# Linear ReLU attention on one core: the first octet's K loaded as 256 pieces of 4 KB into the halves of two output buffers

## The chip, the core and the metric

The kernel runs on one core of one Trainium2 chip. The metric is the device time of one execution in microseconds (us); of three runs the median is 125.16 us (125.11 to 125.23). The core has a matrix engine (PE, with its weight loads PEld), a vector engine (DVE), a scalar engine (ACT), GpSimd (POOL) and a sync engine (SP), and 16 DMA engines that move data between the HBM and the on-chip memory. That memory has 128 partitions. SP and POOL issue all transfers of this kernel, each on a queue of its own; the 16 DMA engines serve both queues.

## The reference

For each of 8 x 12 = 96 heads, with 512 rows of 64 numbers in Q, K and V:

```python
Q_feat = np.maximum(0, Q)
K_feat = np.maximum(0, K)
KV = np.einsum('bhkd,bhkv->bhdv', K_feat, V)
K_sum = np.sum(K_feat, axis=2)
numerator = np.einsum('bhqd,bhdv->bhqv', Q_feat, KV)
denominator = np.einsum('bhqd,bhd->bhq', Q_feat, K_sum)
return (numerator / (denominator[:, :, :, None] + 1e-10)).astype(np.float32)
```

Inputs and output are fp32, 12.58 MB each.

## The kernel before

The heads are taken eight at a time: 12 octets, each 1 MB of Q, K, V and output. An octet of an input is one contiguous megabyte in the HBM; it is laid on the 128 partitions as 128 rows of 2048 fp32, so a partition holds 32 sequence rows of one head (16 partitions for each head).

**Loads.** Of octets 1 to 11, and of octet 0's Q, every load is issued by POOL (`load`, line 171, the transfer on line 174) and converts to bf16 on the way, into rings of six slots for each of Q, K and V (`NI = 6`). Octets 2 to 9 are loaded two at a time, the others singly. Six semaphore lanes (`LANES`) limit how many loads POOL has under way, so POOL runs ahead of the engines that use the data. Octet 0's K and V are the exception: `body` (lines 265 to 267) has SP load them first of all, in fp32, into the output buffers `o_sb[0]` and `o_sb[1]`, which hold no output yet. `kv_src` (line 166) tells the steps that prepare K and V where an octet lies.

**Compute.** For each octet DVE makes `kf` from K (`prep_k`, line 187: the maximum with zero, and a mask that keeps the heads apart), DVE and ACT make `vo` from V (`prep_v`, line 194), and DVE copies Q (`copy_q`). PE transposes Q, sums K against V over 64 matmuls (line 412), multiplies with Q (line 381) and transposes the result back (line 421). DVE scales it by the reciprocal denominators into an output buffer (`norm`, line 241). Octet o's output goes to buffer (o + 2) mod 10 of the ten (`NOUT = 10`) 8 KB buffers.

**Stores.** SP issues the 12 stores of 1 MB (`store`, line 248). Each also waits for the last K load (line 252), so no store starts before all K loads have landed. Those of octets 0 to 3 are issued at the step of octet 4, each later one at the end of its octet's step. After the last store SP waits until its data has landed (line 433), which ends the program.

**Order.** Class `Order` (line 9) keeps, for every buffer key such as `("o", 0)` or `("k", 3)`, its last writer and its readers, and turns them into semaphore waits. The order of instructions on each engine is the order in which `body`, `setup`, `begin` and `step` write them.

Of the kernel before, what the change touches and what calls it, by code (L numbers as in the profile page):

```python
# [96 lines left out]
def kernel(  # L97
# [8 lines left out]
    B, H, S, D = Q.shape  # L106
    assert D == 64
    P = 128
# [3 lines left out]
    R = S * 4 // P  # L112
    RQ = S * 8 // P
# [3 lines left out]
    NI = 6  # L117
    NOUT = 10
    LANES = 6

    fp32 = mybir.dt.float32
    bf16 = mybir.dt.bfloat16
    Act = mybir.ActivationFunctionType
    Alu = mybir.AluOpType

    sb = ctx.enter_context(tc.tile_pool(name="sb", bufs=1))
    psum = ctx.enter_context(tc.tile_pool(name="psum", bufs=1, space=bass.MemoryType.PSUM))

    def view(X, f):
        return X.rearrange("b h s d -> (b h s d)").rearrange("(n p f) -> n p f", p=P, f=f)  # L130

    Qr, Kr, Vr, Or = [view(X, RQ * D) for X in (Q, K, V, out)]
# [3 lines left out]
    mask = sb.tile([P, 2, 2], fp32, name="mask")  # L136
    mask_h = sb.tile([P, 8, 2], fp32, name="mask_h")
    kf = sb.tile([P, RQ, 2, D], bf16, name="kf")
    vo = sb.tile([P, RQ, 2, D4], bf16, name="vo")
# [6 lines left out]
    den = sb.tile([P, RQ], fp32, name="den")  # L146
    rec = sb.tile([P, RQ], fp32, name="rec")
    ins = {n: sb.tile([P, NI, RQ * D], bf16, name=f"{n}_sb") for n in "qkv"}
    o_sb = [sb.tile([P, RQ, D], fp32, name=f"o_sb{i}") for i in range(NOUT)]
    ps_kv = psum.tile([P, 2, 512], fp32, name="ps_kv")  # L150
    ps_den = ps_kv[:, 1, 256:512]
    ps_qt = [psum.tile([P, U // 2, P], bf16, name=f"ps_qt{j}") for j in range(2)]
# [7 lines left out]
    def lane(who):  # L160
        turn[who] += 1
        return lanes[who][(turn[who] - 1) % len(lanes[who])]

    do = Order(nc, sems)

    def kv_src(o):
        if o == 0:
            return (o_sb[0], ("o", 0)), (o_sb[1], ("o", 1))
        return [(ins[n][:, o % NI].rearrange("p (r d) -> p r d", d=D), (n, o % NI)) for n in "kv"]

    def load(n, *octets):
        o, i, m = octets[0], octets[0] % NI, len(octets)
        src = {"q": Qr, "k": Kr, "v": Vr}[n][o:o + m].rearrange("n p f -> p n f")
        do.op("pool", lambda e: e.dma_start(out=ins[n][:, i:i + m], in_=src, single_packet=True),  # L174
              writes=[(n, x % NI) for x in octets], dma=lane("pool"))

    def load_two(o):
        if o < NO - 2:
            load("q", o, o + 1)
            load("k", o, o + 1)  # L180
            load("v", o, o + 1)
        else:
            for x in (o, o + 1):
                for n in "kqv":
                    load(n, x)

    def prep_k(o, s, halves=(0, 1), after=()):
        src, key = kv_src(o)[0]
        rs = slice(R * halves[0], R * halves[-1] + R)
        do.op("dve", lambda e: e.tensor_scalar(kf[:, rs, s, :], src[:, rs], scalar1=0.0, scalar2=mask[:, 0, s:s + 1],  # L190
                                               op0=Alu.max, op1=Alu.mult),
              reads=[key, ("mask", 0), *after], writes=[("kf", s, j) for j in halves])

    def prep_v(o, t, halves, who, sem=None):
        src, key = kv_src(o)[1]
        rs = slice(R * halves[0], R * halves[-1] + R)
        to, src, m = vo[:, rs, t, 2:D + 2], src[:, rs], mask[:, 1, t:t + 1]
        if who == "act":
            make = lambda e: e.activation(to, src, Act.Copy, scale=m)  # L199
        else:  # L200
            make = lambda e: e.tensor_scalar(to, src, scalar1=m, scalar2=None, op0=Alu.mult)  # L201
        do.op(who, make, reads=[key, ("mask", 1), "vo1"], writes=[("vo", t, j) for j in halves], sem=sem)

    def copy_q(o):
        do.op("dve", lambda e: e.tensor_copy(q2.rearrange("p u f -> p (u f)"), ins["q"][:, o % NI]),  # L205
# [33 lines left out]
        do.op("dve", lambda e: e.reciprocal(rec, den), reads=["den"], writes=["rec"])  # L239

    def norm(o, j):
        i = (o + 2) % NOUT
        rs = slice(16 * j, 16 * j + 16)
        do.op("dve", lambda e: e.tensor_tensor(o_sb[i][:, rs], ps_x[j].rearrange("p (r d) -> p r d", d=D),  # L244
                                               rec[:, rs].unsqueeze(2).to_broadcast([P, 16, D]), op=Alu.mult),
              reads=[("x", j), "rec"], writes=[("o", i, j)] if i > 1 else [("o", i, j), ("o", i)], sem=f"n{j}")

    def store(o):
        i = (o + 2) % NOUT
        to, src = Or[o], o_sb[i].rearrange("p r d -> p (r d)")  # L250
        keys = [("o", i, h) for h in range(2)]
        keys.append(("k", (NO - 1) % NI))
        do.op("sp", lambda e: e.dma_start(out=to, in_=src), reads=keys,
              dma=lane("sp" if o + NOUT < NO else "last"), kept=o + NOUT >= NO)
# [6 lines left out]
    def memset(who, ap, value, key):  # L261
        do.op(who, lambda e: e.memset(ap, value), writes=[key] if isinstance(key, (str, tuple)) else key)  # L262

    def body():
        for c, X in enumerate((Kr, Vr)):
            do.op("sp", lambda e: e.dma_start(out=o_sb[c].rearrange("p r d -> p (r d)"), in_=X[0]),
                  writes=[("o", c)], dma=lane("sp"))
        load("q", 0)
        memset("pool", ident, 0.0, "ident")
        do.op("pool", lambda e: e.affine_select(out=ident, in_=ident, compare_op=Alu.not_equal, fill=1.0, base=0,  # L270
                                                pattern=[[-1, P]], channel_multiplier=1),
              reads=["ident"], writes=["ident"])
        for n in "kqv":
            load(n, 1)
        ones = vo[:, :, :, 1:D4 - 1]
        for c in range(4):
            memset("pool", ones[:, 8 * c:8 * c + 8, :, 0:D + 2:D1], 0.0, "vo1")
        for h in range(4):
            for c in range(4):
                memset("pool", ones[32 * h:32 * h + 32, 8 * c:8 * c + 8, h % 2, 0:D + 2:D1], 1.0, "vo1")  # L280
        for h in range(4):
            for t in range(2):
                memset("pool", mask[32 * h:32 * h + 32, 1, t:t + 1], 1.0 if h % 2 == t else 0.0,
                       [("m", h, t), ("mask", 1)])
        setup()
        load_two(2)
        load_two(4)
        begin()
        for o in range(NO):
            step(o)  # L290
        for n in lanes["pool"] + lanes["sp"]:
            nc.gpsimd.wait_ge(sems[n], do.count[n])
        nc.gpsimd.drain()

    def setup():
        do.op("dve", lambda e: e.tensor_copy(ident32, ident), reads=["ident"], writes=["ident32"])
        for c in range(2):
            do.op("dve", lambda e: e.tensor_reduce(
                out=mask_h[:, :, c], in_=ident32.rearrange("p (h b) -> p h b", h=8), op=Alu.add,
                axis=mybir.AxisListType.X), reads=["ident32"], writes=[("mh", c), "mask_h"])  # L300
        do.op("dve", lambda e: e.tensor_reduce(
            out=mask[:, 0, :], in_=mask_h[:, :, 0].rearrange("p (a s) -> p s a", s=2), op=Alu.add,
            axis=mybir.AxisListType.X), reads=["mask_h"], writes=[("mask", 0)])
        prep_k(0, 0)
        prep_k(0, 1)
        prep_v(0, 1, (0,), "act", "a0")
        prep_v(0, 0, (0, 1), "dve", "d0")
        prep_v(0, 1, (1,), "dve", "d1")
        do.op("dve", lambda e: e.memset(kvf.bitcast(fp32)[:, 0:4 * D1], 0.0), writes=KVD, sem="n0")
        do.op("dve", lambda e: e.memset(kvf.bitcast(fp32)[:, 4 * D1:], 0.0), writes=KVD, sem="n1")  # L310
        copy_q(0)
        for who, e, names in (("act", nc.scalar, ("t0", "t1", "rq", "ev")), ("dve", nc.vector, ("n0", "n1"))):
            for n in names:
                e.sem_inc(sems[n], 1)
                do.note(who, who, (), (), n, 1)
# [9 lines left out]
    def prepare(o):  # L325

        copy_q(o)
        for j in range(2):
            prep_k(o, 0, (j,))
            prep_k(o, 1, (j,), ["rec"] if j == 0 else [])  # L330

    def begin():
        transposed(1)
        relu_q(0)
        relu_q(1)
        summed(1)
        evac_kv()
        prep_v(1, 1, (0,), "act", "a0")
        prepare(1)

    def step(i):
# [25 lines left out]
        for j in range(2):  # L367
            norm(i, j)
        if i % 2 == 0 and i + 6 < NO:
            load_two(i + 6)  # L370
            if i + 8 == NO:
                for x in range(i):
                    store(x)
        if i + 8 >= NO:
            store(i)
# [50 lines left out]
    with tc.tile_critical(no_gpsimd_drain=True):  # L426
        body()
        products()
# [34 lines left out]
```

## Time and profile before

| what | value |
|---|---|
| median of three runs | 125.16 us |
| the profiled execution: its own time, its span | 125.21 us, 123.4 us |
| HBM read and written | 37.75 MB, 12.58 MB (408 GB/s over the span) |
| DVE, PE, ACT, POOL busy share of the span | 69%, 66%, 62%, 18% |
| POOL's queue: packets, share of the 16 DMA engines' time | 4704, 71.8% |
| SP's queue: packets, share of the 16 DMA engines' time | 2016, 28.5% |
| octet 0's K, issue to landing | 6.4 us |
| octet 0's V, issue to landing | 10.9 us |
| `prep_k` of octet 0 on DVE | 2 instructions, 2.48 us |

The span is what the profiler saw between the first and the last instruction; the execution's own time has 1.8 us more around it. "Busy" is time in which an engine executed something. The GB/s of the page count the bytes as they arrive: a load that converts 8 KB of fp32 to 4 KB of bf16 counts as 4 KB, so 214 GB/s of such loads read 428 GB/s from the HBM.

The records of single DMA packets in the trace give the size, start and duration of each row moved. SP's rows are 8192 bytes, POOL's 4096 bytes as written. Each of the 16 engines also writes a 4-byte packet to a semaphore when its part of a transfer is done.

### The profile page before, as it was taken

How to read it: one execution, taken by the hardware profiler on the slowest of the kernel's cores; microseconds unless marked ns; L12 is line 12 of the kernel's file. 1: busy time of each engine (PE TensorE's matmuls, PEld its weight loads, DVE VectorE, ACT ScalarE, POOL GpSimd, SP SyncE). 2: the span in 40 equal slices, each digit the busy share in tenths (PEclk: the TensorE clock that was granted, in tenths of full speed). 3: DMA queues.
4: the chain of work that ended last, by engine and by line, in shares of the span. 5: the costliest groups of instructions: out<-in, count | busy, mean ns of one | idle time of the engine just before them, and what ended most of it. 6: DMA issues, size and time to landing. Idle time of an engine off the chain costs nothing.

```text
span 123.4 us, 3445 instructions
## 1 busy us (share of the span) xinstructions
PE 81.2 (66%) x1440; PEld 72.4 (59%) x1440; DVE 85.7 (69%) x149; ACT 76.2 (62%) x108; POOL 21.6 (18%) x56
## 2 busy tenths in 40 slices
PE   0000088793579999898959889597999989390000
PEld 0000077693269789797939789495978977290000
DVE  1252936626975999999989899898999956733000
ACT  0000755991099697999859995799999896300000
POOL 5887922102022022010110110200000000000000
PEclk9999999999756999999999999999999999959555
DMA  2999999999999999999999999999999999999990
GB/s 72 393 313 234 212 214 214 212 212 216 216 212 215 215 216 214 212 216 214 212 215 215 215 215 214 214 215 214 212 324 421 425 425 427 422 425 425 430 425 35
DMA packets 6724, 32.55 MB, mean 264 GB/s; under 512 B 576, under 2 KB 576, under 8 KB 4928
## 3 DMA queue, kind: packets, MB, share of 16 engines
q0 software_dynamic: 4704, 17.83, 71.8%
q1 hardware_dynamic: 2016, 14.68, 28.5%
q8 instruction: 1, 0.02, 0.1%
q14 instruction: 3, 0.02, 0.0%
HBM read 37.75 MB, written 12.58 MB: 408 GB/s over the span
## 4 chain that ended last, share of the span: by engine, by line
DMA 43%; DVE 11%; PE 11%; POOL 11%; issue 9%; ACT 5%; POOLq 0%; DVEq 0%; SPq 0%
DMA v_sb<-in_V_dram 24%; DMA q_sb<-in_Q_dram 20%; DVE o_sb L244 7%; PE ps_x L421 5%; PE ps_kv L412 5%; POOL vo L262 5%; POOL q_sb L174 2%; POOL k_sb L174 2%; DVE vo L201 2%; ACT ot_sb L225 2%; ACT qt L209 1%; DVE own L230 1%; ACT kvd L217 1%; POOL v_sb L174 1%; ACT vo L199 1%
## 5 line engine op out<-in xcount | busy, mean ns | idle before, releaser
L244 DVE TENSOR_TENSOR o_sb<-ps_x,rec 128x1024 f32<-128x1024 f32 x24 | 28.5, 1219 | 5.6 <-PE ps_x L421 5.1
L412 PE MATMUL ps_kv<-vo,kf 64*128 64x132 bf16 x768 | 26.9, 229 | 7.0 <-ACT vo L199 3.5
L412 PEld LDWEIGHTS ps_kv<-vo,kf 64*128 64x128 bf16 x768 | 24.9, 99 | 10.2 <-ACT vo L199 7.8
L421 PE MATMUL ps_x<-ident,ot_sb 128*128 128x128 f32 x192 | 25.4, 289 | 1.7 <-DVE ot_sb L225 1.7
L209 ACT ACTIVATE qt<-ps_qt 128x1024 bf16<-128x1024 bf16 x24 | 23.5, 1040 | 2.1 <-PE ps_qt L388 2.1
L421 PEld LDWEIGHTS ps_x<-ident,ot_sb 128*128 128x128 f32 x192 | 22.6, 149 | 3.3 <-issue 2.2
L388 PE MATMUL ps_qt<-ident,q 128*128 128x128 bf16 x192 | 13.5, 226 | 16.2 <-DVE q L205 15.9
L225 ACT COPY ot_sb<-ps_x 128x1024 f32<-128x1024 f32 x23 | 22.2, 1015 | 2.9 <-PE ps_x L381 2.6
L190 DVE TENSOR_SCALAR kf<-k_sb,mask 128x1024 bf16<-128x1024 bf16 x44 | 19.2, 491 | 6.0 <-DMA k_sb<-in_K_dram 3.5
L388 PEld LDWEIGHTS ps_qt<-ident,q 128*128 128x128 bf16 x192 | 12.2, 101 | 16.5 <-issue 16.3
L217 ACT CAST kvd<-ps_kv 64x260 bf16<-64x260 f32 x48 | 18.0, 375 | 2.2 <-PE ps_kv L412 1.4
L199 ACT ACTIVATE vo<-v_sb,mask 128x1024 bf16<-128x1024 bf16 x11 | 12.7, 1154 | 10.1 <-DMA v_sb<-in_V_dram 9.9
L381 PE MATMUL ps_x<-qt,kvd 128*128 128x256 bf16 x96 | 13.7, 281 | 3.7 <-DVE o_sb L244 3.7
L201 DVE TENSOR_SCALAR vo<-v_sb,mask 128x2048 bf16<-128x2048 bf16 (+1 forms) x22 | 12.6, 617 | 1.3 <-DMA v_sb<-in_V_dram 1.3
L381 PEld LDWEIGHTS ps_x<-qt,kvd 128*128 128x128 bf16 x96 | 8.0, 99 | 6.2 <-DVE o_sb L244 5.0
L205 DVE COPY q<-q_sb 128x2048 bf16<-128x2048 bf16 x12 | 8.1, 674 | 2.1 <-PE ps_qt L388 2.1
L199 ACT ACT_TABLE_LOAD x1 | 1.3, 1283 | 12.4 <-DMA o_sb<-in_V_dram 12.4
L174 POOL DMA_DIRECT2D q_sb<-in_Q_dram x8 | 5.2, 655 | 18.1 <-DMA k_sb<-in_K_dram 8.7
L174 POOL DMA_DIRECT2D k_sb<-in_K_dram x7 | 5.0, 713 | 18.4 <-DMA q_sb<-in_Q_dram 10.1
L174 POOL DMA_DIRECT2D v_sb<-in_V_dram x7 | 4.8, 679 | 19.1 <-DMA v_sb<-in_V_dram 14.5
L381 PE MATMUL ps_kv<-kvd,qt 128*128 128x16 bf16 x192 | 7.0, 179 | 1.3 <-ACT kvd L217 1.3
L381 PEld LDWEIGHTS ps_kv<-kvd,qt 128*128 128x128 bf16 x192 | 6.1, 96 | 2.2 <-ACT kvd L217 2.1
(20 smaller groups left out, 29.5 us busy)
## 6 DMA issues: line engine op xcount, KB each, us to landing
out_dram<-o_sb SPq DMA_DIRECT2D x12, 1024.0 KB, 15.2
q_sb<-in_Q_dram POOLq DMA_DIRECT2D x4, 1024.0 KB, 26.6
k_sb<-in_K_dram POOLq DMA_DIRECT2D x4, 1024.0 KB, 27.9
v_sb<-in_V_dram POOLq DMA_DIRECT2D x4, 1024.0 KB, 29.1
q_sb<-in_Q_dram POOLq DMA_DIRECT2D x4, 512.0 KB, 15.2
k_sb<-in_K_dram POOLq DMA_DIRECT2D x3, 512.0 KB, 19.3
v_sb<-in_V_dram POOLq DMA_DIRECT2D x3, 512.0 KB, 15.5
o_sb<-in_K_dram SPq DMA_DIRECT2D x1, 1024.0 KB, 6.4
```

What stands on the lines that cost most here:

```text
L174: do.op("pool", lambda e: e.dma_start(out=ins[n][:, i:i + m], in_=src, single_packet=True), writes=[(n, x % NI) for x in octets], dma=lane ...
L190: do.op("dve", lambda e: e.tensor_scalar(kf[:, rs, s, :], src[:, rs], scalar1=0.0, scalar2=mask[:, 0, s:s + 1], op0=Alu.max, op1=Alu.mult) ...
L199: make = lambda e: e.activation(to, src, Act.Copy, scale=m)
L201: make = lambda e: e.tensor_scalar(to, src, scalar1=m, scalar2=None, op0=Alu.mult)
L209: do.op("act", lambda e: e.activation(qt[:, j * (U // 2):(j + 1) * (U // 2)], ps_qt[j], Act.Relu), reads=[("pq", j)], writes=[("qt", j)], ...
L217: do.op("act", lambda e: e.copy(kvd[64 * c:64 * c + 64, s:8:2, c * D1:c * D1 + D1].rearrange("p (g t) d -> p g t d", t=2), ps_kv[64 * s:64 ...
L225: do.op(who, lambda e: e.copy(to, src) if who == "act" else e.tensor_copy(to, src), reads=[("x", j)], writes=[("ot", j)], sem=f"t{j}")
L244: do.op("dve", lambda e: e.tensor_tensor(o_sb[i][:, rs], ps_x[j].rearrange("p (r d) -> p r d", d=D), rec[:, rs].unsqueeze(2).to_broadcast( ...
L381: return pe.matmul(out_, lhsT, rhs, start=True, stop=True, skip_group_check=True)
L388: x = pe.transpose(ps_qt[u // 8][:, u % 8, :], q2[:, u, :], ident)
L412: x = pe.matmul(ps_kv[:, h, 0:2 * (D + 2)].rearrange("p (t d) -> p t d", t=2), kf[ps, R * g + k, :, :].rearrange("p s d -> p (s d)"), vo[p ...
L421: x = pe.transpose(ps_x[u // 8][:, u % 8 * P:u % 8 * P + P], ot[:, u].rearrange("p h c -> p (h c)"), ident32)
```

## The change

Octet 0's K goes to the first 4 KB of output buffer 0 and the first 4 KB of output buffer 1, instead of the whole of buffer 0: each partition's 8 KB is cut into two halves of 1024 fp32. V moves from buffer 1 to buffer 2. For this the ten buffers become one tile. `prep_k` reads its source as halves `j`, for octet 0 from the two buffers, for the others from the ring slot as before. The outputs move on by one buffer, to (o + 3) mod 10, and the extra key that orders an output behind octet 0's inputs is now on buffers 0 to 2. In the built program the K transfer's memory side has 256 rows of 1024 fp32, and its on-chip side 128 x 2 x 1024; before, both had 128 rows of 2048.

```diff
-    o_sb = [sb.tile([P, RQ, D], fp32, name=f"o_sb{i}") for i in range(NOUT)]
+    o_all = sb.tile([P, NOUT, RQ * D], fp32, name="o_sb")
+    o_sb = [o_all[:, i].rearrange("p (r d) -> p r d", d=D) for i in range(NOUT)]
+
+    k_first = o_all[:, 0:2, 0:R * D]
...
     def kv_src(o):
         if o == 0:
-            return (o_sb[0], ("o", 0)), (o_sb[1], ("o", 1))
-        return [(ins[n][:, o % NI].rearrange("p (r d) -> p r d", d=D), (n, o % NI)) for n in "kv"]
+            return (k_first, [("o", 0), ("o", 1)]), (o_sb[2], [("o", 2)])
+        return (ins["k"][:, o % NI].rearrange("p (j f) -> p j f", j=2), [("k", o % NI)]), (
+            ins["v"][:, o % NI].rearrange("p (r d) -> p r d", d=D), [("v", o % NI)])
...
     def prep_k(o, s, halves=(0, 1), after=()):
-        src, key = kv_src(o)[0]
-        rs = slice(R * halves[0], R * halves[-1] + R)
-        do.op("dve", lambda e: e.tensor_scalar(kf[:, rs, s, :], src[:, rs], scalar1=0.0, scalar2=mask[:, 0, s:s + 1],
-                                               op0=Alu.max, op1=Alu.mult),
-              reads=[key, ("mask", 0), *after], writes=[("kf", s, j) for j in halves])
+        src, keys = kv_src(o)[0]
+        js = slice(halves[0], halves[-1] + 1)
+        to = kf.rearrange("p (j r) s d -> p j r s d", j=2)[:, js, :, s, :]
+        do.op("dve", lambda e: e.tensor_scalar(to, src[:, js].rearrange("p j (r d) -> p j r d", d=D), scalar1=0.0,
+                                               scalar2=mask[:, 0, s:s + 1], op0=Alu.max, op1=Alu.mult),
+              reads=[*keys, ("mask", 0), *after], writes=[("kf", s, j) for j in halves])
...
     def norm(o, j):
-        i = (o + 2) % NOUT
+        i = (o + 3) % NOUT
...
-              reads=[("x", j), "rec"], writes=[("o", i, j)] if i > 1 else [("o", i, j), ("o", i)], sem=f"n{j}")
+              reads=[("x", j), "rec"], writes=[("o", i, j)] if i > 2 else [("o", i, j), ("o", i)], sem=f"n{j}")
...
     def store(o):
-        i = (o + 2) % NOUT
+        i = (o + 3) % NOUT
...
     def body():
-        for c, X in enumerate((Kr, Vr)):
-            do.op("sp", lambda e: e.dma_start(out=o_sb[c].rearrange("p r d -> p (r d)"), in_=X[0]),
-                  writes=[("o", c)], dma=lane("sp"))
+        do.op("sp", lambda e: e.dma_start(out=k_first, in_=Kr[0].rearrange("p (j f) -> p j f", j=2)),
+              writes=[("o", 0), ("o", 1)], dma=lane("sp"))
+        do.op("sp", lambda e: e.dma_start(out=o_all[:, 2], in_=Vr[0]), writes=[("o", 2)], dma=lane("sp"))
```

More of the change, by code (lines that the diff above doesn't have):

```diff
@@ L187, in prep_k @@
     def prep_k(o, s, halves=(0, 1), after=()):
-        src, key = kv_src(o)[0]
-        rs = slice(R * halves[0], R * halves[-1] + R)
-        do.op("dve", lambda e: e.tensor_scalar(kf[:, rs, s, :], src[:, rs], scalar1=0.0, scalar2=mask[:, 0, s:s + 1],
-                                               op0=Alu.max, op1=Alu.mult),
-              reads=[key, ("mask", 0), *after], writes=[("kf", s, j) for j in halves])
+        src, keys = kv_src(o)[0]
[4 more added lines that the diff above has]
+              reads=[*keys, ("mask", 0), *after], writes=[("kf", s, j) for j in halves])
     def prep_v(o, t, halves, who, sem=None):
-        src, key = kv_src(o)[1]
+        src, keys = kv_src(o)[1]
         rs = slice(R * halves[0], R * halves[-1] + R)
@@ L201, in prep_v @@
             make = lambda e: e.tensor_scalar(to, src, scalar1=m, scalar2=None, op0=Alu.mult)
-        do.op(who, make, reads=[key, ("mask", 1), "vo1"], writes=[("vo", t, j) for j in halves], sem=sem)
+        do.op(who, make, reads=[*keys, ("mask", 1), "vo1"], writes=[("vo", t, j) for j in halves], sem=sem)
     def copy_q(o):
```

## The prediction

> **What bounds the kernel now.** First I read the table of busy time by stretches, cut where the character of the transfers changes. Its columns are the stretch, its length, busy time and instructions of PE, PEld, DVE, ACT and POOL, the granted clock, the DMA share and GB/s.
>
> ```profile
> 0.00:2.00 2.00, 0.00 (x0) 0.00 (x0) 0.00 (x0) 0.00 (x0) 0.76 (x5) 1.00 0.07 8
> 2.00:3.00 1.00, 0.00 (x0) 0.00 (x0) 0.23 (x2) 0.00 (x0) 0.92 (x4) 1.00 0.54 188
> 3.00:5.00 2.00, 0.00 (x0) 0.00 (x0) 0.73 (x3) 0.00 (x0) 1.89 (x6) 1.00 0.99 410
> ...
> 10.00:80.00 70.00, 54.11 (x994) 48.49 (x996) 55.50 (x100) 52.19 (x74) 13.88 (x30) 0.95 1.06 214
> ...
> 92.00:120.00 28.00, 15.83 (x244) 13.71 (x241) 15.43 (x25) 12.31 (x18) 0.00 (x0) 0.84 1.01 425
> 120.00:121.00 1.00, 0.00 (x0) 0.00 (x0) 0.00 (x0) 0.00 (x0) 0.00 (x0) 0.50 0.51 213
> 121.00:122.00 1.00, 0.00 (x0) 0.00 (x0) 0.00 (x0) 0.00 (x0) 0.00 (x0) 0.50 0.10 41
> ```
>
> From 3 to 120 us the DMA engines never rest, while no compute engine is full. The trace's packet records say the same row by row: each engine starts a new 8 KB row of SP's every 306 ns, and a new POOL row every 308 ns (104 starts in 2 us over 16 engines). An engine has (2 + 12) x 8 = 112 SP rows and 34 x 8 = 272 POOL rows: 112 x 0.306 + 272 x 0.308 = 118 us. Begun at about 2.6 us, that ends at 120.6. So it does: most engines end between 120.3 and 121.1, and two stragglers at 121.71 and 121.98. The last landing is at 122.45, and the span ends 1.0 us later.
>
> Next, who waits at the end, and where the compute chain takes its time from: the SP queue's waits and the chain of waits.
>
> ```profile
> SPq L434 <- DMA out_dram<-o_sb: 9.2, 1, 9.2
> ```
> ```profile
> 48.72 29.06 DMA v_sb<-in_V_dram
> 77.78 0.02 issue
> 77.80 1.16 ACT vo L199
> ```
>
> Compute waits for a V load until 77.78 us, so its clock is set there by the transfers, whatever happened at the start. And SP sits 9.2 us behind the last store. That store is issued at 112.39. The first store took 3.2 us from its issue (87.63) to its first row (90.88), with other rows ahead of it; 3.2, eight rows (2.45) and 0.46 to land make 118.5 us, against 122.45. So compute has 3.9 us to spare at the end. **The end is the start of the first rows plus all rows of the slowest DMA engine.** The change can move either of these two.
>
> **Part 1: the issue of K.** What stands ahead of the first row:
>
> ```profile
> 0.96 0.39 SPq L266 DMA_DIRECT2D o_sb<-in_K_dram  x1
> 1.40 0.42 SPq L266 DMA_DIRECT2D o_sb<-in_V_dram  x1
> ```
>
> SP issues K from 0.96 to 1.35. First rows appear at 1.98 to 2.09 on four engines and at 2.58 to 2.90 on the other twelve. POOL's rows follow only at 5.35. Until the first rows nothing covers the issue: a longer one moves all work of the DMA engines. How much longer for 256 pieces? The nearest rows are POOL's issues of one octet (128 rows) and of two (256 pieces):
>
> ```profile
> 3.71 0.55 POOL L174 DMA_DIRECT2D v_sb<-in_V_dram  x1
> ...
> 11.85 0.71 POOL L174 DMA_DIRECT2D q_sb<-in_Q_dram  x1
> ```
>
> They give +0.16 us for 128 more pieces, or a factor of 1.29, which on 0.386 us is +0.11. The bounds: nothing, if the first pieces leave while the others are being made, and +0.39, if the whole issue doubles. Below nothing it can hardly go, as K's issue does strictly more. I take +0.20, a little above POOL's row, for a reason in the built program. There 13 of SP's 14 transfers (V and the stores) have the same two-dimensional pattern on both sides and carry a mark of a pattern prepared ahead; K had both and loses both, with 256 x 1024 on one side and 128 x 2 x 1024 on the other. What SP then has to work out itself no row here shows, so the choice is mine and the bounds stay. V's issue comes later by as much; it is covered, since V's first row is due only after K's eight rows (2.45 us).
>
> [...]
>
> **Part 2: the pieces on the DMA engines.** Eight rows of 8 KB on each engine become 16 pieces of 4 KB; the bytes are the same. The 4-byte semaphore packet of SP's queue gives the fixed part of a packet: 9 ns (beside rows of 309) while SP's rows run alone, 22 ns (beside rows of 322) when they alternate with POOL's. A line through 4 bytes and 8192 bytes puts a 4 KB piece at 159 or 172 ns, so two pieces cost 9 or 22 ns more than the row. Times eight: +0.07 or +0.18 us on each engine, the bounds. Fifteen of 16 engines finish K before POOL's rows arrive, so I take a value near the first, +0.09. The Trainium skill, "DMA: Bandwidth & Descriptors", section "Why small descriptors are slow (HBM only)", states about 3 cycles over 32-byte beats for each packet: 131 against 128 beats for a piece. By it I estimate 8 x 309 ns x (262/259 - 1) = 0.03 us, a third of the row's 9 ns for each piece, and the sum below would be 0.06 less.
>
> **Part 3: what is hidden.** `prep_k` of octet 0 now reads two runs of 1024 instead of one of 2048: two instructions of 1.28 us, between unchanged and doubled (+2.56). DVE is idle for 2.43 us after them, waiting for V, so at most 0.13 us would show there, and that only delays compute. For later octets the built instructions have the same patterns as before. The outputs' shift by one buffer gives octet 7 a wait between its two `norm` instructions that octets 8 and 9 have already; their starts are 1.26 us apart where others' are 1.14, so it costs 0.12 us of DVE time at about 83 us. K itself may land later: one engine moves a 16 KB instruction packet for 1.02 us from 4.75, its last K rows then alternate with POOL's, and K lands at 7.37 instead of 5.7. As 4 KB pieces each of those rows lets one more POOL row past, some 0.3 us for each of two or three rows: up to 0.9 us for K and for V behind it (landed at 12.29). Queued behind them are DVE's preparation, `copy_q` and PE's first transposes (15.9 us). All of it goes into the compute slack: the loads set compute's clock at 77.78, and 3.9 us remain at the end. POOL's loads run ahead by six lanes (a median of 27 us from issue to landing for the large ones), so they do not starve. Price at the end: 0; uncovered, up to 0.9.
>
> **Sum.** +0.20 + 0.09 = +0.29 us. On the profiled execution's own 125.21 us (span 123.4) that is 125.50. This execution is 0.05 above the median of the runs shown, so I forecast 125.45 us.
>
> **The rivals.** The bound of what a measurement here can tell is 0.2%, or 0.25 us.
>
> B, no difference: the first pieces leave as they are made, and only part 2 is left, 125.16 + 0.09 = 125.25. For it: rows of four engines appear 0.5 us before the others', so transfers do start before everything is ready. Against it: POOL's 0.55 and 0.71 us. If the pieces were merged back into rows of 8 KB, it would be 125.16; the gap of 4 KB between the halves speaks against that.
>
> C, faster: the first rows are the slow ones. On the four early engines they took 1120, 1074, 932 and 894 ns, later ones 309. If an engine has to receive a whole piece before it passes it on, a half-sized first piece saves up to half of the excess, (1005 - 309) / 2 = 0.35 us, and with part 2 the end is at 124.90. This decides if the issue term is small and the engine that ends last is among those four. Against it: the other twelve have first rows of 307 to 399 ns and all 16 are at their second row between 2.9 and 3.2 us, which leaves half of a row, 0.15 us, for 125.10.
>
> D, much slower: the longer issue feeds the engines one after another. Before, first rows are spread over 0.93 us (1.98 to 2.90). If the spread doubles, an engine served late starts up to 0.93 us later, and if it is one of the two stragglers the end is 125.16 + 0.93 + 0.09 = 126.18. For it: the spread exists. Against it: the ends of first rows are spread over 0.3 us only.
>
> **How the numbers follow.** Forecast (issue +0.11 to +0.39, pieces +0.07 to +0.18, so 125.34 to 125.73, most of it over the bound of 125.41): 0.50. B with the merged pieces: 0.24. C: 0.17, of which 0.14 over the bound. D: 0.09. Slower by over 0.2%: 0.43 of the forecast's 0.50 and D, 0.52. Faster: 0.14, to which I add 0.04, taken from B, for a straggler of the DMA engines that fares better after any shift; 0.18. Within: the remaining 0.30. For eight times in ten the range has to reach B and part of C and D: 124.90 to 126.00.
>
> **What would show it.** Right: SP's issue of K at about 0.5 to 0.6 us; the bulk of first rows at 2.7 to 2.9 instead of 2.58; K's pieces at about 159 ns; rows of 306 and 308 ns and no gap afterwards; the last landing later by the same amount as the first rows plus 0.1. Wrong: an issue of 0.39 us (B); first rows ending earlier than 2.9 us (C); first rows spread over more than 1.5 us (D); a DMA share below 0.99 anywhere between 3 and 120 us, or a last store whose landing follows its issue within 7 us, which would put compute at the end.

## The result, and the profile after

The changed kernel takes 125.75 us (median of six runs, 125.47 to 126.06), the kernel before beside it 125.17 us. The ratio is 1.0049 with a 95% interval of [1.0033, 1.0065]: 0.58 us slower. The forecast was 125.45 us. Run again on two other occasions, each beside the kernel before, the changed kernel gave 1.0026 [1.0015, 1.0038] and 1.0047 [1.0030, 1.0064], so the size is 0.36 to 0.58 us by these medians.

The profiled execution took 125.67 us with a span of 123.9, against 125.21 and 123.4 before. First the issues on SP, from the timeline (start, duration):

```profile
0.97 0.65 SPq L270 DMA_DIRECT2D o_sb<-in_K_dram  x1
1.67 0.57 SPq L272 DMA_DIRECT2D o_sb<-in_V_dram  x1
```

K's issue is 0.65 us instead of 0.39. V's grew as well, from 0.42 to 0.57, though V's transfer has the pattern it had. Next the table by stretches, with the columns as before:

```profile
0.00:2.00 2.00, 0.00 (x0) 0.00 (x0) 0.00 (x0) 0.00 (x0) 0.76 (x5) 1.00 0.00 0
2.00:3.00 1.00, 0.00 (x0) 0.00 (x0) 0.23 (x1) 0.00 (x0) 0.93 (x4) 1.00 0.26 41
3.00:5.00 2.00, 0.00 (x0) 0.00 (x0) 0.74 (x3) 0.00 (x0) 1.89 (x6) 1.00 0.90 342
10.00:80.00 70.00, 53.50 (x982) 48.33 (x984) 55.41 (x101) 51.69 (x73) 14.03 (x28) 0.98 1.06 215
92.00:120.00 28.00, 14.59 (x246) 12.37 (x244) 15.70 (x26) 12.59 (x19) 0.00 (x0) 0.88 1.02 427
120.00:121.00 1.00, 0.00 (x0) 0.00 (x0) 0.00 (x0) 0.00 (x0) 0.00 (x0) 0.50 0.93 393
121.00:122.00 1.00, 0.00 (x0) 0.00 (x0) 0.00 (x0) 0.00 (x0) 0.00 (x0) 0.50 0.20 82
```

What is lost stands in the first 5 us: 41 GB/s instead of 188 from 2 to 3 us, and 342 instead of 410 from 3 to 5. From 10 to 120 us the rates are the old ones, and at the end the missing work is still there, 393 GB/s from 120 to 121 us instead of 213. By the packet records 0.1 MB had been read by 3.70 us (before 3.17), 4 MB by 13.04 (12.46), 20 MB by 50.42 (49.85), and the last landing is at 122.90 (122.45). A delay of 0.53 us arises ahead of the first 0.1 MB and is carried through all loads (0.58 us at 4 MB, 0.57 at 20 MB); at the last landing 0.45 is left of it.

Compute is no nearer to the end than before. The SP queue's waits:

```profile
SPq L439 <- DMA out_dram<-o_sb: 10.6, 1, 10.6
```

SP now waits 10.6 us for the last stores instead of 9.2; the last one was issued at 111.48 us, earlier than before (112.39).

### The profile page after: what moved, and what is told of

It reads as the page before. It is cut to its first block, busy times and chain, and to the rows that moved or that the text cites. A ratio compares the mean times of both kernels' runs of the same rounds, so it can differ in the third digit from the quotient of the medians.

```text
span 123.9 us, 3446 instructions
## 1 busy us (share of the span) xinstructions
PE 79.3 (64%) x1440; PEld 71.1 (57%) x1440; DVE 85.6 (69%) x149; ACT 76.1 (61%) x108; POOL 21.7 (17%) x56
## 4 chain that ended last, share of the span: by engine, by line
DMA 40%; DVE 17%; PE 15%; POOL 8%; ACT 6%; issue 3%; POOLq 0%; DVEq 0%; SPq 0%
DMA v_sb<-in_V_dram 40%; DVE o_sb L249 12%; PE ps_kv L417 9%; PE ps_x L426 5%; POOL vo L267 4%; DVE vo L206 2%; ACT vo L204 2%; DVE own L235 2%; ACT ot_sb L230 2%; ACT qt L214 1%; POOL q_sb L178 1%; ACT kvd L222 1%; POOL k_sb L178 1%; DVE ot_sb L230 1%; POOL mask L267 1%
## 5 line engine op out<-in xcount | busy, mean ns | idle before, releaser
L417 PE MATMUL ps_kv<-vo,kf 64*128 64x132 bf16 x768 | 27.5, 231 | 7.6 <-ACT vo L204 4.6
L417 PEld LDWEIGHTS ps_kv<-vo,kf 64*128 64x128 bf16 x768 | 25.5, 101 | 10.6 <-ACT vo L204 8.3
L426 PE MATMUL ps_x<-ident,ot_sb 128*128 128x128 f32 x192 | 23.5, 275 | 1.7 <-DVE ot_sb L230 1.7
L426 PEld LDWEIGHTS ps_x<-ident,ot_sb 128*128 128x128 f32 x192 | 20.8, 140 | 3.3 <-issue 2.0
L386 PE MATMUL ps_x<-qt,kvd 128*128 128x256 bf16 x96 | 13.1, 273 | 2.9 <-DVE o_sb L249 2.9
L210 DVE COPY q<-q_sb 128x2048 bf16<-128x2048 bf16 x12 | 7.6, 635 | 2.1 <-PE ps_qt L393 2.1
L178 POOL DMA_DIRECT2D v_sb<-in_V_dram x7 | 5.3, 762 | 19.1 <-DMA v_sb<-in_V_dram 10.3
L178 POOL DMA_DIRECT2D k_sb<-in_K_dram x7 | 4.5, 636 | 18.4 <-DMA q_sb<-in_Q_dram 10.1
```

What stands on the lines that cost most here:

```text
L386: return pe.matmul(out_, lhsT, rhs, start=True, stop=True, skip_group_check=True)
L417: x = pe.matmul(ps_kv[:, h, 0:2 * (D + 2)].rearrange("p (t d) -> p t d", t=2), kf[ps, R * g + k, :, :].rearrange("p s d -> p (s d)"), vo[p ...
L426: x = pe.transpose(ps_x[u // 8][:, u % 8 * P:u % 8 * P + P], ot[:, u].rearrange("p h c -> p (h c)"), ident32)
```

## The experiments

The table gives, for each run, the time, the kernel before beside it, the ratio with its interval, SP's first issue, the first row on any DMA engine, the time by which 0.1 MB had been read, and the last landing (the last four from each run's profiled execution, in us).

| run | us | before | ratio | issue | first row | 0.1 MB | last landing |
|---|---|---|---|---|---|---|---|
| kernel before | 125.17 | | | 0.39 | 1.98 | 3.17 | 122.45 |
| changed kernel | 125.75 | 125.17 | 1.0049 [1.0033, 1.0065] | 0.65 | 2.40 | 3.70 | 122.90 |
| rest8k | 125.22 | 125.22 | 1.0003 [0.9993, 1.0013] | 0.39 | 1.99 | 3.11 | 122.45 |
| unprep8k | 125.56 | 125.21 | 1.0028 [1.0019, 1.0037] | 0.55 | 2.30 | 3.45 | 122.65 |
| unprep8k_b | 125.65 | 125.23 | 1.0041 [1.0027, 1.0055] | 0.55 | 2.31 | 3.51 | 122.83 |
| after2 | 125.58 | 125.22 | 1.0026 [1.0015, 1.0038] | 0.65 | 2.42 | 3.59 | 122.81 |
| after3 | 125.72 | 125.23 | 1.0047 [1.0030, 1.0064] | 0.65 | 2.41 | 3.54 | 122.99 |
| pieces2k | 125.54 | 125.21 | 1.0031 [1.0022, 1.0040] | 0.65 | 2.39 | 3.50 | 122.69 |
| vfirst | 125.35 | 125.21 | 1.0012 [1.0003, 1.0021] | 0.39 | 1.99 | 3.21 | 122.45 |
| vfirst8k | 125.30 | 125.22 | 1.0005 [0.9996, 1.0014] | 0.39 | 1.99 | 3.22 | 122.26 |
| vpieces2k | 125.66 | 125.23 | 1.0043 [1.0028, 1.0058] | 0.39 | 1.99 | 3.32 | 122.91 |
| two4k | 125.87 | 125.21 | 1.0054 [1.0041, 1.0068] | 0.39 | 1.99 | 2.86 | 123.19 |
| vtwo4k | 125.77 | 125.22 | 1.0043 [1.0030, 1.0057] | 0.39 | 1.99 | 3.10 | 123.10 |
| actv | 125.36 | 125.23 | 1.0011 [1.0001, 1.0020] | 0.38 | 1.95 | 3.19 | 122.58 |

### The change without its transfer: rest8k

```diff
-    k_first = o_all[:, 0:2, 0:R * D]
+    k_first = o_all[:, 0].rearrange("p (j f) -> p j f", j=2)
...
-        do.op("sp", lambda e: e.dma_start(out=k_first, in_=Kr[0].rearrange("p (j f) -> p j f", j=2)),
-              writes=[("o", 0), ("o", 1)], dma=lane("sp"))
+        do.op("sp", lambda e: e.dma_start(out=o_all[:, 0], in_=Kr[0]), writes=[("o", 0), ("o", 1)], dma=lane("sp"))
```

> Everything of the change but the transfer: one tile for the ten buffers, V in buffer 2, outputs moved on by one buffer, prep_k reading by halves; K itself in 128 rows of 8 KB into buffer 0, with the mark. Theory (the time is lost ahead of the first rows and in K's transfer alone): issue 0.39 us, first rows at 2.0 and 2.6 us, 125.2 us. Rival (buffers, waits and reads cost part of it): 125.4 us or more.

125.22 us beside 125.22. The buffers, the extra wait of octet 7 and the reads by halves cost nothing that can be measured (the interval ends at 0.16 us), so the loss is in K's transfer.

### The lost mark alone: unprep8k, unprep8k_b and after3

The kernel before, built with K's transfer (the one for c = 0) kept off the prepared path:

```diff
         for c, X in enumerate((Kr, Vr)):
+            nc.dge_precook = c > 0
             do.op("sp", lambda e: e.dma_start(out=o_sb[c].rearrange("p r d -> p (r d)"), in_=X[0]),
                   writes=[("o", c)], dma=lane("sp"))
```

> The kernel before, with K in 128 rows of 8 KB as it was; only the mark of a pattern prepared ahead is left out of K's transfer when the program is built. Theory (SP's longer issue of K starts every DMA engine late, and the lost mark is why it is longer): SP's issue of K about 0.65 us as in the changed kernel instead of 0.39, first rows 0.4 to 0.5 us later than before, the end as much later: about 125.65 us. Rival (the 256 pieces are why: twice as many to make): issue 0.39 to 0.45 us, first rows as before, 125.2 us.

It took 125.56 us. The rival is out: rows of 8 KB, as many as before, are 0.35 us slower once the mark is gone. The timeline of SP:

```profile
0.97 0.55 SPq L267 DMA_DIRECT2D o_sb<-in_K_dram  x1
1.58 0.57 SPq L267 DMA_DIRECT2D o_sb<-in_V_dram  x1
```

The issue is 0.55 us, not the 0.65 that the theory expected: the mark is worth 0.16, and the other 0.10 of the changed kernel belongs to something else in its pattern. It also shows where V's longer issue comes from: 0.57 us here too, so it follows an unmarked transfer, not the pieces. The first row comes 0.78 us after the issue's end, before 0.63. So the lost mark costs 0.16 us in the issue and 0.15 behind it. No trace shows the mark itself, only what goes with it: V's issue of 0.57 to 0.59 us stands behind K in this run, in the changed kernel and in pieces2k below, and 0.43 behind the marked K of rest8k.

The changed kernel had first come out 0.23 us further from its control than this run from its own. That the two had not stood beside each other left open whether the pieces cost as much as the mark. These two runs put them together:

> Rows of 8 KB without the mark, again, now beside the changed kernel on one chip. The question is what the changed kernel adds to the lost mark. Theory (nearly nothing but 0.10 us of longer issue): 125.5 to 125.6 us, and the changed kernel up to 0.15 above it. Rival (the pieces and their pattern are half of the cost, as the first measurement of 0.58 us against 0.35 would have it): the changed kernel 0.2 to 0.3 us above it.

> The changed kernel, as the partner of rows of 8 KB without the mark. Theory: 125.55 to 125.7 us; rival: 125.75 us or more with the other at 125.5.

125.65 and 125.72 us, beside 125.23; both are just above their expected ranges. By these medians the mark costs 0.42 us and the rest of the transfer 0.07. The two intervals overlap widely, so the 0.07 is not told from nothing; that the mark is the larger part holds in both sessions.

### More and smaller pieces: pieces2k

K over four buffers instead of two (V in the fifth, outputs moved on by five); K's lines of the edit:

```diff
-    k_first = o_all[:, 0:2, 0:R * D]
+    k_first = o_all[:, 0:4, 0:R * D // 2]
...
-        do.op("sp", lambda e: e.dma_start(out=k_first, in_=Kr[0].rearrange("p (j f) -> p j f", j=2)),
-              writes=[("o", 0), ("o", 1)], dma=lane("sp"))
+        do.op("sp", lambda e: e.dma_start(out=k_first, in_=Kr[0].rearrange("p (j f) -> p j f", j=4)),
+              writes=[("o", j) for j in range(4)], dma=lane("sp"))
...
```

`prep_k` reads octet 0's K in four parts here.

> The changed kernel with K in 512 pieces of 2 KB, in the first quarters of four output buffers (V in the fifth, outputs moved on by five buffers). Theory (the lost mark costs once, whatever the number of pieces): issue 0.65 to 0.7 us, first pieces as in the changed kernel, 16 more pieces on each engine at some 3 ns each: 125.8 us. Rival (time to make the pieces): issue about 1.2 us, first pieces another 0.5 us later, 126.3 us.

125.54 us, 0.26 below the theory, though its issue came out as expected. SP's timeline:

```profile
0.97 0.65 SPq L271 DMA_DIRECT2D o_sb<-in_K_dram  x1
1.67 0.59 SPq L273 DMA_DIRECT2D o_sb<-in_V_dram  x1
```

512 pieces take SP no longer than 256 (0.646 and 0.645 us), and the first row is at 2.39 us as well. Between these two the number of pieces is not in the issue. The 0.10 us over the 0.55 of rows without the mark goes with the unequal pattern of three dimensions that both kernels have; nothing was run that separates its parts. The time missed the theory at the other end: by the packet records this run was 0.53 us behind the kernel before at 20 MB (50.38 against 49.85 us), nearly as far as the changed kernel's 0.57, but its last landing is only 0.24 us later. How the last engine gives time back is taken up under "The sum" below.

### V ahead of K: vfirst and vfirst8k

```diff
-        do.op("sp", lambda e: e.dma_start(out=k_first, in_=Kr[0].rearrange("p (j f) -> p j f", j=2)),
-              writes=[("o", 0), ("o", 1)], dma=lane("sp"))
         do.op("sp", lambda e: e.dma_start(out=o_all[:, 2], in_=Vr[0]), writes=[("o", 2)], dma=lane("sp"))
+        do.op("sp", lambda e: e.dma_start(out=k_first, in_=Kr[0].rearrange("p (j f) -> p j f", j=2)),
+              writes=[("o", 0), ("o", 1)], dma=lane("sp"))
```

> The changed kernel with V's transfer issued ahead of K's. Theory (the end is the start of the first rows plus all rows): V's issue takes 0.4 us from 0.96, its rows start at 2.0 to 2.9 us as K's did before, K's longer issue lies behind V's 2.45 us of rows, and only the pieces are left: 125.2 to 125.3 us, though K lands some 5 us later. Rival (the changed kernel's time is lost elsewhere than ahead of the first rows): 125.75 us. Rival (the late K delays compute to the end): above 125.75 us, with a last store whose landing follows its issue within 7 us.

125.35 us, 0.14 above the kernel before and just above the range expected. SP's timeline, then DVE's:

```profile
0.97 0.39 SPq L270 DMA_DIRECT2D o_sb<-in_V_dram  x1
1.42 0.63 SPq L271 DMA_DIRECT2D o_sb<-in_K_dram  x1
```
```profile
14.94 2.63 DVE L195 TENSOR_SCALAR kf<-o_sb,mask 128x2048 bf16<-128x2048 f32 x2 [11.13 <-DMA o_sb<-in_K_dram]
```

K's slow issue is all there, 0.63 us, but behind V's rows, and most of the loss is gone (0.14 us, where the changed kernel gave 0.36 to 0.58). DVE gets K 7.5 us later than in the kernel before (7.47), and that costs 0.14 us at most: the compute slack at the start is real. What is left should be the pieces, or the late K. The control:

> The kernel before with V's transfer ahead of K's, both in rows of 8 KB and with the mark. It is the control for V issued first in the changed kernel (which took 125.35 us): the difference of the two is what K's 256 pieces cost once their issue is covered. Theory: the order alone costs nothing, 125.2 us, and the pieces 0.05 to 0.15. Rival (the late K is what cost 0.14 us there): 125.35 us here too.

1.0005 [0.9996, 1.0014] against 1.0012 [1.0003, 1.0021]. The difference, 0.0007 or 0.09 us, would be the pieces; the intervals overlap, so these two runs alone do not settle it. Nor does the control decide between its theory and its rival: it stands 0.08 us above its own kernel before, half way between none and 0.14.

### The pieces three times over: vpieces2k

The kernel of pieces2k with V's line ahead of K's.

> V first, then K in 512 pieces of 2 KB: the pieces' own cost three times over (384 more pieces than rows, where the changed kernel has 128 more), with the issue covered. Theory (a piece more costs 6 ns alone and up to 22 ns beside POOL's rows, so 24 more on each engine cost 0.15 to 0.5 us, and the covered issue nothing): 125.4 to 125.7 us. Rival (pieces are free while POOL's rows run beside them): 125.25 us, as with rows of 8 KB.

1.0043, against 1.0005 with rows of 8 KB in another session: 0.0038 or 0.48 us for 24 more pieces on each engine, 20 ns each. By the packet records the run is 0.36 us behind vfirst8k at 20 MB (50.30 against 49.94 us), 15 ns each. Pieces are not free, and the single packets point the same way: 309, 159 and 84 ns for 8, 4 and 2 KB while SP's rows run alone, 322, 172 and 96 beside POOL's. That makes 4 x 96 - 322 = 62 ns more for each of eight rows, 0.50 us; it is an upper figure, because beside POOL's rows the records overlap a little (DMA shares up to 1.09 in the tables below). The late K is not the cost: its preparation starts only at 19.68 us, but SP waits 10.4 us behind the last store, as long as in vfirst (10.1).

### Two marked transfers of half rows: two4k and vtwo4k

```diff
-        do.op("sp", lambda e: e.dma_start(out=k_first, in_=Kr[0].rearrange("p (j f) -> p j f", j=2)),
-              writes=[("o", 0), ("o", 1)], dma=lane("sp"))
+        for j in range(2):
+            do.op("sp", lambda e: e.dma_start(out=k_first[:, j], in_=Kr[0][:, j * R * D:(j + 1) * R * D]),
+                  writes=[("o", j)], dma=lane("sp"))
```

> The changed kernel, with K's 256 pieces of 4 KB to the same places but as two transfers of 128 pieces each (first halves, then second halves), each with the same two-dimensional pattern on both sides and with the mark. Theory: the first issue is 0.39 us again, first rows as in the kernel before, and only the pieces' own cost is left, 156 against 306 ns for a row, 8 x 6 ns = 0.05 us: 125.2 us. Rival (4 KB pieces are slow on the DMA engines, or the buffers, waits and split reads of the change cost the time): as the changed kernel, 125.75 us.

A miss: 125.87 us, slower than the changed kernel, though the issue was 0.39 us and 0.1 MB was read by 2.86 us, earlier than in any other run. The loss comes next. The changed kernel read from 0.25 to 0.5 MB in 0.62 us, this one in 1.09. Of its 109 pieces that started before 4 us, 51 took 200 to 560 ns, the others about 160; of the changed kernel's 70 it was 12. It reads the same 4 KB pieces, but every second one first. Is that a matter of the start alone? vtwo4k puts V ahead of these two transfers:

> V first, then K's 256 pieces as two marked transfers of 128 (first halves, then second halves). In the two transfers without V ahead, the pieces took 200 to 560 ns each until 4 us, and about 0.5 us was lost between 0.25 and 0.5 MB. Theory (reading every second 4 KB of a memory that was not touched before is slow only as long as nothing else is there to read): with V's rows ahead and POOL's beside them the pieces run at 160 to 172 ns, 125.3 to 125.4 us. Rival (every second 4 KB is slow whenever it is read): pieces of over 200 ns again, 125.6 us or more.

The rival's time held, 125.77 us, but not its pieces. The tables by stretches, first of vtwo4k, then of vfirst, whose one transfer names the same pieces in the order of memory:

```profile
6.00:7.00 1.00, 0.00 (x0) 0.00 (x0) 0.00 (x0) 0.00 (x0) 0.77 (x5) 1.00 0.97 233
7.00:8.00 1.00, 0.00 (x0) 0.00 (x0) 0.00 (x0) 0.70 (x1) 0.71 (x6) 1.00 0.89 205
8.00:9.00 1.00, 0.00 (x0) 0.00 (x0) 0.00 (x0) 0.58 (x1) 0.71 (x6) 1.00 1.12 229
9.00:10.00 1.00, 0.00 (x0) 0.00 (x0) 0.00 (x0) 0.00 (x0) 0.66 (x8) 1.00 0.97 246
10.00:11.00 1.00, 0.00 (x0) 0.00 (x0) 0.00 (x0) 1.00 (x1) 1.00 (x2) 1.00 1.06 299
```
```profile
6.00:7.00 1.00, 0.00 (x0) 0.00 (x0) 0.00 (x0) 0.00 (x0) 0.77 (x5) 1.00 1.02 274
7.00:8.00 1.00, 0.00 (x0) 0.00 (x0) 0.00 (x0) 0.27 (x1) 0.71 (x6) 1.00 1.09 287
8.00:9.00 1.00, 0.00 (x0) 0.00 (x0) 0.00 (x0) 1.00 (x1) 0.71 (x6) 1.00 0.98 274
9.00:10.00 1.00, 0.00 (x0) 0.00 (x0) 0.00 (x0) 0.01 (x1) 0.66 (x8) 1.00 1.06 291
10.00:11.00 1.00, 0.00 (x0) 0.00 (x0) 0.00 (x0) 1.00 (x1) 1.00 (x2) 1.00 1.11 291
```

From 6 to 9 us, while the first halves are read, vtwo4k moves 205 to 233 GB/s and vfirst 274 to 287. It is not K's pieces themselves that take long (176 to 180 ns on average), but POOL's rows beside them: 370, 387 and 425 ns on average in these three microseconds, against 322. From 10 us on, when the second halves are read, everything runs at the full rate. Why the first pass is slow is open: the two kernels differ in the order of the pieces, but also in the number of transfers and in the mark, and no run separates these. For the change it means that its one transfer spares a loss which another way to cut K into 4 KB pieces has.

### The changed kernel again, and a try for less: after2 and actv

> The changed kernel once more, beside the others on one chip. Theory (of its 0.58 us, 0.35 is what the lost mark cost alone with rows of 8 KB; the rest is 0.10 for issuing the pattern of 256 rows and what the pieces cost): issue 0.65 us, 0.1 MB read by 3.5 to 3.7 us instead of 3.2, 125.6 to 125.8 us. If it comes out at 125.5 us or less, the pieces cost nothing beside the issue.

125.58 us: just below the range expected, 0.36 us above the kernel before. The 0.1 MB were read by 3.59 us, as expected.

The try, from the kernel before:

```diff
-        for c, X in enumerate((Kr, Vr)):
-            do.op("sp", lambda e: e.dma_start(out=o_sb[c].rearrange("p r d -> p (r d)"), in_=X[0]),
-                  writes=[("o", c)], dma=lane("sp"))
+        do.op("sp", lambda e: e.dma_start(out=o_sb[0].rearrange("p r d -> p (r d)"), in_=Kr[0]),
+              writes=[("o", 0)], dma=lane("sp"))
+        do.op("act", lambda e: e.dma_start(out=o_sb[1].rearrange("p r d -> p (r d)"), in_=Vr[0]),
+              writes=[("o", 1)], dma=lane("sp"))
```

> A try for less time than both: the kernel before, with V's transfer issued by ACT at the same time as K's by SP, both with rows of 8 KB. If the first rows of some engines wait for the issue, two queues at once bring 0.1 to 0.3 us: 124.9 to 125.1 us. Theory: the engines have K's rows to read by 2.6 us anyway, V's issue was covered, so no difference: 125.2 us.

1.0011 [1.0001, 1.0020]: no gain, and 0.13 us more rather than the same. ACT's rows of V start at 1.95 us, and SP's first K row only at 2.99 behind them. No version that was run beats the kernel before.

## Why the prediction was right, and where its sizes were off

**The bound.** Right. The rows keep their pace after the start, compute has slack on both sides (K 7.5 us late in vfirst, SP 10.6 us behind the last store), and each kernel that starts its rows late ends late. It is not the only way to end late: two4k and vtwo4k start early and lose their time in the rows, which is the other half of the bound.

**Part 1, the issue: right in place and direction, too small in size.** The forecast was +0.20 us ahead of the first rows. The runs show +0.26 in the issue itself, +0.16 more between its end and the first row (0.63 to 0.79 us), and in all 0.42 at the first row and 0.37 to 0.53 at 0.1 MB. I had priced only what the issue row shows, and had not put a term for what follows it. The row that I took the price from was also the wrong one: POOL's 0.55 and 0.71 us count pieces, and on SP the count costs nothing (256 and 512 pieces alike). What I added for the lost mark was a guess, and it is the largest part: by itself the mark cost 0.35 and 0.42 us. That the upper bound of +0.39 was to cover the first rows' delay failed too; 0.42 lies beyond it. Two signs named for "right" were missed with it: the issue is 0.65 us and not 0.5 to 0.6, and in the changed kernel's first profile only four pieces start at 2.40 to 2.45 us and all others from 2.93 us on, not at 2.7 to 2.9.

**Part 2, the pieces: right.** The line through the semaphore packet foresaw 159 and 172 ns for 4 KB; the packets took 159 and 172, and at 2 KB 84 and 96. K ran almost alone, as assumed, where starts follow each other by 156 ns instead of 306 for a row: 8 x (2 x 156 - 306) = 0.05 us of the forecast's 0.09. The estimate of 0.03 us from the Trainium skill, "DMA: Bandwidth & Descriptors", section "Why small descriptors are slow (HBM only)", is nearer to these 0.05 than my 0.09. It comes to 3.6 ns for each row (four tenths of the 9 ns, not a third), where the starts show 6. Beside another queue's rows the trace does not agree with it: there a piece more cost 15 to 20 ns (vpieces2k). In the time of the changed kernel itself 0.05 us cannot be told from nothing.

**Part 3, what is hidden: right in price, not in the way it was argued.** rest8k shows nothing. K's preparation began at 7.85 us instead of 7.47 and V's at 12.77 instead of 12.38, less than half of the 0.9 us allowed for. In after2 they began at 7.44 and 12.35, no later than in the kernel before. In the changed kernel's three profiles one K piece at the end ran beside POOL's rows (172 ns, started between 6.50 and 6.92 us), the pieces just before it alone (159 ns). The 16 KB instruction packet, behind which more of them were to alternate, had moved (see below).

**The sum.** +0.29 against 0.58 in the first measurement, and 0.36 and 0.49 in the others. The bounds of the two terms end at 125.73 us; the first measurement lies just above, the repeats (125.58 and 125.72) within. That the stated range reaches 126.00 is owed to rival D, which did not come true, so the first measurement's place in the range is in part luck. The start gave more than foreseen, and the last engine gave a little back. The engine that moves the 16 KB instruction packet did so at 2.35 us in the changed kernel, ahead of its first K piece, and no longer in the middle of K at 4.75. The last 4-byte packet of most engines moved by 0.5 to 0.8 us (from about 120.45 to 121.2), that of the last engine by 0.45 (121.98 to 122.43). After2, after3 and pieces2k have the packet at 2.33 to 2.34 us too, and all other runs at 4.57 to 5.53. It would also account for pieces2k, 0.53 us behind at 20 MB and 0.24 at the end. That the packet and the last engine belong together is argued from the times, as the records do not name the engine, and why the packet moved is open.

**The rivals.** B fell with the issue of 0.65 us. The Trainium skill, "DMA: Bandwidth & Descriptors", section "Anatomy of one DMA — SWDGE (gpsimd) path", says of transfers that GpSimd issues that many descriptors can be emitted before their cost shows. POOL's issues do not agree (0.55 us for 128 pieces, 0.71 for 256), and for SP's the section says nothing; there 256 and 512 pieces take the same, and what unprep8k shows is a cost of another kind. C: in the first profile of the changed kernel the first pieces were shorter on the early engines (536 to 649 ns instead of 894 to 1120). In after2 and after3 all but one of the first 15 pieces took 644 to 1181 ns, about what the first whole rows of rest8k took (516 to 1186), so a first piece of half the size need not take half the time. D: the first pieces were not spread further (2.40 to 3.25 us, and one at 3.79 behind the instruction packet; in after2 and after3 the first 15 start within 0.3 us). How many engines start early differs between runs of the same transfer: four in the kernel before, twelve in rest8k, with 0.1 MB read at 3.17 and 3.11 us. So the time of the 0.1 MB is the safer mark of the start. One sign that I had named as "wrong" did appear, a DMA share of 0.90 from 3 to 5 us; it is the start itself, which reached past 3 us.

## What to carry to other kernels

When the DMA engines are full from the first row to the last, what is lost ahead of the first row is paid at the end (the changed kernel was 0.37 to 0.53 us late at 0.1 MB and 0.36 to 0.54 us at the last landing). So is what makes the rows themselves slower (vpieces2k, vtwo4k), while lateness in compute was covered. Put the transfer that is quickest to issue first, and the odd one behind its rows. Compare the issue of a transfer and the gap to its first row, not only bytes and pieces. In this build a pattern that differs between its two sides left the prepared path without a word in the source; the built program shows it.

## What the runs showed of the hardware that was not expected

- An SP transfer that is not prepared ahead costs 0.16 us more in its issue, 0.15 us more until its first row, and 0.15 us in the issue of the marked transfer behind it (0.42 to 0.57).
- 512 pieces take SP as long to issue as 256 (0.646 and 0.645 us).
- While one transfer read the first 4 KB of every 8 KB of a megabyte, the rows of another queue went from 322 to as much as 425 ns on average; while a second transfer read the other halves, they did not. The cause is open.
- One or two DMA engines end 1 to 1.5 us after most others (121.71 and 121.98 against about 120.45 us in the kernel before), and the last alone sets the end. The trace has one 16 KB instruction packet (1.02 us in the kernel before), a delay that only one engine has.
